# Another layout, and whole rows of 64, for the rotary part of q between two stages of a transformer kernel

## The chip, the cores and the metric

The kernel runs on one core of one Trainium2 chip, as one launch. The metric is the device time of a run in microseconds. Within the core, TensorE (PE in the profile; its weight loads are the row PEld), VectorE (DVE), ScalarE (ACT) and GpSimd (POOL) compute, SyncE (SP) issues every DMA of this kernel, and sixteen DMA engines move the data.

## The reference, cut to what matters

The program is a block of three parts on 1024 tokens of 1024 features: layer 0 (differential attention), layer 1 (attention with compressed keys and queries, "MLA"), and a second block (three mixers and a feed-forward part). Only layer 1 is touched:

```python
def _mla(h, positions, w_in, q_a_norm_g, w_q_b, kv_a_norm_g, w_kv_b, w_out):
    proj = h @ w_in
    q_a, c_kv, k_pe, z = jnp.split(proj, [384, 640, 704], axis=-1)
    q = (_rmsnorm(q_a, q_a_norm_g) @ w_q_b).reshape(b, s, 8, 128 + 64)
    q_nope = q[..., :128]
    q_pe = _rope(q[..., 128:], positions)            # 64 features of each of 8 heads
    k_pe = _rope(k_pe[:, :, None, :], positions)[:, :, 0]   # 64 features, shared by the heads
    kv = (_rmsnorm(c_kv, kv_a_norm_g) @ w_kv_b).reshape(b, s, 8, 128 + 128)
    k_nope, v = kv[..., :128], kv[..., 128:]
    # per head: softmax((q_nope . k_nope + q_pe . k_pe) * 192 ** -0.5) @ v
    o = o.reshape(b, s, 1024) * jax.nn.silu(z)
    return o @ w_out
```

(The sizes are written in for the constants.) `_rope` turns the 64 features of a row in pairs (feature f of the first half with feature f of the second half, f from 0 to 31).

## The kernel before

All arithmetic is fp32; for the matmuls each operand is split into two parts, hi and lo, whose sum is exact, and a product takes three of the four part products (the scores of the rotary part take all four). Activations are kept transposed, features on the partitions, in token halves of 512. A tile has 4 KB a partition; pools hand out a fixed number of buffers for each tag and phase.

Layer 1 runs like this. `lora_norm` makes the normalised q_a and c_kv. `mla_kpe` (L998) makes the rotary part of k for all tokens, stacks hi over lo on 128 partitions and stores it in the DRAM scratch `kd` (L1017); it is read back once into the tile `kpe` (L1142; `h` in the profile, which leaves the digit of the tag `h4` out). `mla_qpe` (L1019) makes the rotary part of q for the heads in two groups of four, g = 0 and 1. A group gives four tiles of 128 partitions, the first and second half of the features (i) by hi and lo (hl); partition 32 x head + f holds feature f. Each tile is stored in the DRAM scratch `qpe` (L1043), which is laid out [head, hl, 64 features, token]: one DMA of 512 KB writes four pieces of 32 rows, one for each head.

Then come eight heads. `mla_head` (L1051) makes q_nope and k_nope of a head, and for hi and for lo it loads the head's 64 rows of `qpe` into a tile of 128 partitions (L1062): one DMA of 512 KB that reads the 64 rows twice, as [2 copies, 64, 1024], so that they stand against the hi rows and against the lo rows of `kpe`. The scores of a query tile are the five matmuls L1093 to L1097 for each half of the keys; L1096 and L1097 use the two loaded tiles. A row maximum on DVE (L737), an exponential on ACT (L741), a scaling on POOL (L1099), transposes on PE (L757), copies to SBUF on ACT and DVE (L761, L169), and the product with v (L192) follow; L1104 multiplies the result by the gate.

While the attention of head h runs, `merge` interleaves v of this head, the preparation of head h + 1 and the modulation vectors of the second block (`modulation`, L298: 48 loads of 512 KB into the three `tb` buffers at L308, and one DVE operation on each, L316 or L318). A scheduler orders the instructions of each engine by its own estimate of the times; each engine, SP too, works through its list in order. SP's DMAs go round eight semaphores, and the next DMA on a semaphore is issued after the last one on it has landed.

Of the kernel before, what the change touches and what calls it, by code (L numbers as in the profile page):

```python
# [44 lines left out]
def alternate(a, b):  # L45
    """steps of a and of b together"""
    for _ in a:
        next(b, None)
        yield
    yield from b  # L50
# [7 lines left out]
def ahead(tc, gen, offset):  # L58
    """steps of gen, scheduled before work that was emitted up to offset instructions earlier"""
    if not offset:  # L60
        yield from gen
        return
    while True:
        with tc.high_priority(offset):
            x = next(gen, drain)
        if x is drain:
            return
        yield x


def some(g, n):
    """n steps of g"""
    for _ in range(n):
        if next(g, drain) is drain:
            return
        yield


def merge(main, fill, lead=0):
    """emit one step of fill after each step of main"""  # L80
    for _ in range(lead):
        next(fill, None)
    for _ in main:
        next(fill, None)
    drain(fill)


def pace(main, total, early, fill, n):
    """steps of early at once, then n steps of fill spread over main, whose steps give their weight"""
    w = done = 0  # L90
    for x in main:
        w += x or 1
        if next(early, 0) == 0:
            while done < n * w / total:
                next(fill, None)
                done += 1
    drain(early)
    drain(fill)


class Net:
# [18 lines left out]
    def load(self, tag, shape, dt=F32):  # L120
        """a tile to be loaded, but not long before its phase"""
        n = self.loads.get((self.phase, tag), 0)
        self.loads[self.phase, tag] = n + 1
        t = self.t(tag, shape, dt)
        if self.phase and n < CAPS[self.phase][tag]:
            first = t[:, 0:1]
            while len(first.shape) > 2:
                first = first[:, :, 0]
            self.nc.gpsimd.tensor_copy(first, self.sign)
        return t  # L130

    def t(self, tag, shape, dt=F32):
        """a tile of 4 KB a partition, seen in the shape"""
        self.n += 1
        t = self.pools[self.phase][tag].tile([128, 1024], dt, tag=f"{tag}{self.phase}", name=f"{tag}_{self.n}")
        dims = "abcd"[:len(shape) - 1]
        t = t[:, 0:math.prod(shape[1:])]
        return t.rearrange(f"p ({' '.join(dims)}) -> p {' '.join(dims)}", **dict(zip(dims, shape[1:])))
# [9 lines left out]
    def c(self, shape, name, dt=F32):  # L148
        """a constant, or columns that stay"""
        r = dt == F32R  # L150
        n = 1 if r else shape[1]
        if name not in self.where:
            self.where[name] = self.used[r]
            self.used[r] += n
        o = self.where[name]
        return self.cr[:, o] if r else self.cf[:, o:o + n]

    def small(self, cols, tag):
        """columns for a short time: the next of a few in turn"""
# [11 lines left out]
    def wblock(self, src, k, m, lo_eng=None):  # L171
        """src: DRAM [k*128, m]; returns [(hi, lo)] per contraction chunk, each [128, m]"""
        return self.wload([src], k, m, lo_eng)

    def wload(self, srcs, k, m, lo_eng=None):
        """blocks of columns side by side"""
# [10 lines left out]
    def mm3(self, out, ws, rs, start=True, stop=True):  # L187
        """out += sum_k ws[k]^T rs[k]; ws, rs: (hi, lo)"""
# [26 lines left out]
    def columns(self, tile_name, width, names):  # L215
        """vectors as columns [128, j]"""
# [23 lines left out]
    def mask_tile(self, name, op, pattern, mult):  # L240
        """0 where the condition holds, else -BIG"""
# [39 lines left out]
    def sigmoid(self, sg, z, src):  # L281
        """sg <- sigmoid(z); src: where |z| is read from (z or its PSUM source)"""
# [15 lines left out]
    def modulation(self, cs, w, bcol, names, acc_tag="t2", w_tag="wr", shared=()):  # L298
        """columns [128, 8] of each 1024 outputs of cs @ w + b; chunks in shared: on ScalarE and GpSimd"""
# [27 lines left out]
    def sum_cols(self, acc, out):  # L327
        """out [128, 8] <- sums over the partitions of acc"""
# [7 lines left out]
    def modulation_first(self, cs, w, bcol, g, nme, acc_tag, w_tag):  # L336
        """as modulation, half of the products on TensorE"""
# [24 lines left out]
    def scale_col(self, g, scale, name):  # L362
        """g * (1 + scale)"""
# [14 lines left out]
    def stat_sum(self, acc):  # L378
        """sum over partitions, on every partition (PSUM)"""
# [10 lines left out]
    def rsqrt_mean(self, out, sums, dim):  # L390
        """(sums / dim + eps)^-1/2"""
# [5 lines left out]
    def stat_end(self, acc, dim):  # L397
        """acc -> (sum over partitions / dim + eps)^-1/2 on every partition, in place"""
        return self.rsqrt_mean(acc, self.stat_sum(acc), dim)

    def new_xt(self, tags):
        """x^T of a token half: 8 chunks [128, 512] in len(tags) tiles"""
# [37 lines left out]
    def operand(self, x, tag="h4", eng=None):  # L440
        """x [128, 512], split"""
# [5 lines left out]
    def rows(self, w, c0, m=128):  # L447
        """loads columns c0.. of w as the rows of a block, by halves of the contraction"""
# [8 lines left out]
    def weights(self, load, early):  # L457
        """operands of two blocks of rows by the number of the product, the first two products' first"""
# [20 lines left out]
    def strassen(self, load, ops, box, tag, early=False):  # L479
        """two blocks of rows times h, [128, 1024] each; early: the products of the first token half, alone,  # L480
        in steps"""
# [31 lines left out]
    def next_h(self, proj, xbox, acc, acol, shift):  # L513
        """ends the projection; h of the next part (fp32, in the place of x), and the operands of its first
        token half"""
# [16 lines left out]
    def turn_ops(self, ops, b11, b12, b21, b22):  # L532
        """operands of a chunk of each half of the contraction, but the first two products'; in place"""
# [11 lines left out]
    def start_pairs(self, pair, n, chunk, ops):  # L545
        """the first pairs of blocks: what needs the first token half, the other operands, the rest"""
# [13 lines left out]
    def load_x(self):  # L560
        """tokens of x"""
# [8 lines left out]
    def turn_x(self, toks):  # L570
        """x^T of the token halves, and their normalisation as rows on every partition"""
# [31 lines left out]
    def rope_half(self, psa, psb, half, outs):  # L603
        """outs: Ah, Al, Bh, Bl views"""
# [15 lines left out]
    def qk_rope(self, w, qcol, kcol, hts, perm=1):  # L620
        """q, k of two 64-wide heads, roped, split and stacked for the scores: kk[s], q[s](hl, q tile)"""
# [56 lines left out]
    def score(self, ps, q, j, kk, ks, stop=True):  # L678
        """ps = q tile j . keys ks, all four products of the parts"""
# [4 lines left out]
    def v_tiles(self, w, cols, k, rs, perm=1, pair=False):  # L684
        """v [key, 128] of the columns, split: [128, hl, 8, 128], or pair: [128, 8, 2, hl, 64]"""
# [31 lines left out]
    def silu_blocks(self, w, cols, hts, box):  # L717
        """silu(h @ w[:, c:c + 128])^T for c in cols, fp32 [128, 1024]"""
# [14 lines left out]
    def exp_row(self, ps, scale):  # L733
        """softmax numerator and reciprocal of its sum"""
# [13 lines left out]
    def pt_fill(self, pts, p, slot, ktiles):  # L748
        """transposes of p[:, k tiles] into column slot; pts = [hi 0-1, lo 0-1, hi 2-3, ..]"""
# [14 lines left out]
    def pv(self, v, pts):  # L764
        """O^T [128, 512]"""
# [5 lines left out]
    def out_proj(self, w, ots, gcol, xs_in, xs_out, half, tags, stats, accs, box):  # L771
        """x' = x + gate * (o @ w) for a token half, in T layout; stats: column factors (or None) of accs"""
# [18 lines left out]
    def keep_o(self, o):  # L791
        """o^T chunk, split"""
# [11 lines left out]
    def load_o(self, od, half, cs, ots, fac=None):  # L804
        """chunks cs of o^T of a token half from DRAM, split"""
# [17 lines left out]
    def last_head(self, att, w0, w1, early, loads, proj, hold=0):  # L823
        """the attention of the last head; fill in its first half (of weight w0): early and the loads of
        the first half's o^T, in its second: the output projection of the first half (but hold steps,
        which come with the loads of the second half's o^T)"""
# [142 lines left out]
    def lora_norm(self, w, c0, n, dim, gcol, hts, tags, box):  # L969
        """rmsnorm of h @ w[:, c0:c0+128n], as (hi, lo) tiles [half][block]"""  # L970
# [28 lines left out]
    def mla_kpe(self, w, c0, hts, kd):  # L999
        """roped k_pe^T stacked [hi (x1, x2); lo (x1, x2)]"""  # L1000
# [16 lines left out]
        nc.sync.dma_start(kd, kpe.bitcast(F32))  # L1017

    def mla_qpe(self, wq, qa, qpe):  # L1019
        """roped q_pe of all heads -> DRAM [head, hl, 64, 1024]"""  # L1020
        nc = self.nc
        for g in range(2):
# [18 lines left out]
            for i in range(2):  # L1041
                for hl in range(2):
                    nc.sync.dma_start(qpe[g * 4:g * 4 + 4, hl, i * 32:i * 32 + 32, :], ab[i][hl].bitcast(F32))  # L1043

    def split_psum(self, ps, dst):
        """dst [128, 2, 512] <- exact parts of ps"""
# [3 lines left out]
    def mla_head(self, h, wq, wkv, qa, ckv, qpe, box):  # L1050
# [9 lines left out]
        for hl in range(2):  # L1060
            t = self.t("h4", [128, S], F32R)
            nc.sync.dma_start(t.bitcast(F32), qpe[h, hl:hl + 1].to_broadcast([2, 64, S]))  # L1062
# [44 lines left out]
    def layer1(self, hts):  # L1107
# [27 lines left out]
        qpe = self.scratch([8, 2, 64, S], "qpe")  # L1135
# [65 lines left out]
    def gelu(self, ps, dst):  # L1201
        """tanh-form gelu of ps into dst (SBUF)"""
# [11 lines left out]
    def mixer_a(self, w, hts, od):  # L1214
        nc, a = self.nc, self.a
        # causal w_sp, transposed and split
# [12 lines left out]
        for b in range(2):  # L1229
# [6 lines left out]
            # v: [s, g, n, c], group norm  # L1236
# [41 lines left out]
    def mixer_b_qk(self, w, p, hts, box):  # L1278
        """q, k of the heads of pair p"""
# [26 lines left out]
    def fold(self, ps, y, e):  # L1306
        """y rows of head e <- sum of the two row halves of ps"""
# [55 lines left out]
    def mixer_c_attention(self, g, d, kk, q, vbox, lse, od):  # L1363
# [4 lines left out]
        for e in range(2):  # L1368
# [61 lines left out]
            # lse = max * scale + ln(sum), 1 / sum; to token order  # L1430
# [17 lines left out]
    def alphas_c(self, lse, fac):  # L1448
        """softmax of lse over the 3 groups, over the softmax sum; [6, 1024] in token order"""
# [80 lines left out]
    def ffn(self, hs, ops):  # L1530
        """the convolved gate and val in pairs of blocks, and their product, kept in DRAM; then the product
        with w_down"""
# [47 lines left out]
    def down(self, half, k1, k2, act, ys):  # L1580
        """x + gate * (act @ w_down) for a token half, in T layout; ys: the chunks before k1"""
# [39 lines left out]
    def finish(self, xt, half):  # L1621
        """rmsnorm of x in token layout, with g_final"""
# [68 lines left out]
```

## Time and profile before

| | |
|---|---|
| median of 3 runs | 3095.03 us (3091.07 to 3096.7) |
| span of the profiled execution | 3102.5 us |
| granted TensorE clock, mean over the span | 0.929 |
| layer 1, from the store of `kd` to the end of the last head | about 1046 to 1620 us of the span |
| DMA issues of the program / of `qpe` and `kd` | 1073 / 8 stores and 16 loads, 1 store and 1 load, 512 KB each |

The span is 7.5 us longer than the median of the runs, and 5.8 us longer than the longest of them. A profile gives the time at which an instruction ran, not what the DMA engines did for it; when a transfer landed is read from the instruction that waited for it. In a timeline row the bracket is the idle time of the engine before the instruction, and what ended it. In a row of windows, "PEclk" is the granted clock and "DMA share" the mean busy share of the sixteen DMA engines.

### The profile page before, as it was taken

The numbers are of one execution on the slowest core, as the hardware profiler recorded it, in microseconds if no ns is written. First come the engines' busy times: TensorE is split into PE (matmuls) and PEld (weight loads), VectorE is DVE, ScalarE is ACT, GpSimd is POOL, SyncE is SP. The second block draws the span as 40 slices with busy tenths as digits, with TensorE's granted clock in tenths as the row PEclk, the third lists the DMA queues.
The fourth block names the chain that finished last, engine by engine and source line by source line (L and its number), as shares of the span: only waits on it lengthen the run. The fifth ranks groups of instructions, "written<-read, shape, count | busy, mean of one in ns | idle before, by whom it ended". The sixth has DMA issues, their size and how long they took to land. (4 is left out here: it accounts for less than half of the span.)

```text
span 3102.5 us, 34630 instructions
## 1 busy us (share of the span) xinstructions
PE 2673.2 (86%) x12023; PEld 2154.1 (69%) x12023; DVE 2110.7 (68%) x2888; ACT 1434.4 (46%) x2609; POOL 1292.2 (42%) x775
## 2 busy tenths in 40 slices
PE   7899999999989957778789689888887999998897
PEld 4677777777767746567667567777675777776776
DVE  7787778766653365555566756377876888889865
ACT  5455554556444423334345444366743444444332
POOL 2323333223353522112124333244545877787761
PEclk8999999999999978889899899999998999998998
DMA  7433333224441352321334235533361222224664
GB/s 268 132 93 96 105 94 90 72 67 118 122 122 53 117 178 78 100 83 53 103 106 131 68 81 82 107 82 100 97 195 46 77 82 75 82 89 149 210 213 153
DMA packets 316225, 338.90 MB, mean 109 GB/s; under 512 B 37060, under 2 KB 239892, under 8 KB 316052
## 3 DMA queue, kind: packets, MB, share of 16 engines
q1 hardware_dynamic: 316052, 336.69, 37.0%
q8 instruction: 96, 1.57, 0.2%
q14 instruction: 77, 0.63, 0.1%
HBM read 231.17 MB, written 60.89 MB: 94 GB/s over the span
## 5 line engine op out<-in xcount | busy, mean ns | idle before, releaser
L192 PE MATMUL m<-h,wh 128*128 128x512 f32 x4744 | 1399.6, 404 | 59.3 <-ACT wh L183 18.6
L192 PEld LDWEIGHTS m<-h,wh 128*128 128x128 f32 x4744 | 912.1, 195 | 269.3 <-ACT wh L183 21.0
L192 PE MATMUL m<-h,wl 128*128 128x512 f32 x1472 | 590.3, 403 | 10.1 <-POOL wl L169 10.0
L169 POOL TENSOR_TENSOR wl<-wr,wh 128x1024 fp32r<-128x1024 f32 (+1 forms) x146 | 329.4, 2263 | 577.6 <-PE m L192 184.4
L761 ACT CAST pt<-m 128x256 fp32r<-128x256 f32 (+1 forms) x632 | 221.2, 369 | 367.8 <-DVE pt L169 192.1
L192 PEld LDWEIGHTS m<-h,wl 128*128 128x128 f32 x1472 | 286.5, 195 | 75.3 <-POOL wl L169 12.5
L169 DVE TENSOR_TENSOR pt<-m,pt 128x256 fp32r<-128x256 f32 (+2 forms) x652 | 256.8, 416 | 103.2 <-ACT pt L761 81.7
L741 ACT ACTIVATE e<-s,cf 128x1024 f32<-128x1024 f32 x192 | 214.8, 1120 | 163.6 <-DVE cf L738 140.2
L737 DVE TENSOR_REDUCE cf<-s 128x1 f32<-128x1024 f32 x192 | 232.6, 1218 | 70.6 <-PE s L682 38.6
L757 PE MATMUL m<-cr,e 128*128 128x128 f32 x1240 | 197.1, 285 | 61.3 <-DVE t L1104 31.4
L757 PEld LDWEIGHTS m<-cr,e 128*128 128x128 f32 x1240 | 155.3, 147 | 89.4 <-issue 53.4
L192 PE MATMUL s<-h,wh 128*128 128x512 f32 x720 | 182.8, 399 | 35.9 <-DVE h L169 17.1
L865 POOL TENSOR_SCALAR e<-e,cf 128x1024 f32<-128x1024 f32 x64 | 82.0, 1281 | 303.8 <-DVE cf L742 286.6
L681 PE MATMUL s<-kk,qq 128*128 128x512 f32 (+3 forms) x376 | 154.0, 415 | 51.6 <-ACT e L741 22.4
L1527 DVE SCALAR_TENSOR_TENSOR e<-z,cf,e 128x1023 f32<-128x1023 f32 (+1 forms) x88 | 175.8, 2008 | 24.8 <-ACT e L1525 24.6
L183 ACT CAST wh<-wr 128x1024 fp32r<-128x1024 f32 (+2 forms) x134 | 122.2, 915 | 145.5 <-PE m L192 67.6
L192 PE MATMUL m<-pt,v 128*128 128x512 f32 x768 | 187.7, 394 | 0.8 <-DVE pt L169 0.6
L192 PEld LDWEIGHTS s<-h,wh 128*128 128x128 f32 x720 | 136.3, 191 | 71.8 <-DVE h L169 18.9
L192 PEld LDWEIGHTS m<-pt,v 128*128 128x128 f32 x768 | 143.9, 189 | 31.6 <-DVE pt L169 1.5
L1099 POOL TENSOR_SCALAR e<-e,cf 128x1024 f32<-128x1024 f32 x64 | 72.8, 1141 | 213.8 <-DVE cf L742 210.0
L682 PE MATMUL s<-kk,qq 128*128 128x512 f32 (+3 forms) x376 | 146.0, 396 | 0.2 <-DMA qq<-pt 0.2
L169 DVE TENSOR_TENSOR wh<-wl,wh 128x512 fp32r<-128x512 f32 x90 | 120.6, 1358 | 19.1 <-ACT wh L443 19.0
(368 smaller groups left out, 4582.3 us busy)
## 6 DMA issues: line engine op xcount, KB each, us to landing
wr<-in_w_out_dram SPq DMA_DIRECT2D x48, 512.0 KB
tb<-in_w_ada_dram SPq DMA_DIRECT2D x48, 512.0 KB
wr<-in_w_up_dram SPq DMA_DIRECT2D x47, 512.0 KB
wr<-in_w_in_dram SPq DMA_DIRECT2D x45, 512.0 KB
qq<-ab SPq DMA_DIRECT2D x144, 128.0 KB
wr<-in_ada_w_dram SPq DMA_DIRECT2D x32, 512.0 KB
tf<-act SPq DMA_DIRECT2D x30, 512.0 KB
wr<-in_w_down_dram SPq DMA_DIRECT2D x30, 512.0 KB
```

Of the source, the lines that this page charges most:

```text
L169: (eng or self.nc.vector).tensor_sub(lo, src, hi.bitcast(F32))
L183: nc.scalar.copy(hi, raw)
L192: self.nc.tensor.matmul(out, l, r, start=start and n == 0, stop=stop and n == last)
L681: nc.tensor.matmul(ps, q(0, j), kk[:, ks], start=True, stop=False)
L682: nc.tensor.matmul(ps, q(1, j), kk[:, ks], start=False, stop=stop)
L737: nc.vector.reduce_max(nm, ps, axis=AX, negate=True)
L741: nc.scalar.activation(e, ps, AF.Exp, bias=nm, scale=scale, accum_out=sm)
L757: nc.tensor.transpose(ps[:, i], p[:, kt * 128:(kt + 1) * 128], self.ident)
L761: nc.scalar.copy(hi, ps[:, i:i + m])
L865: nc.gpsimd.tensor_scalar(e1, e1, r1, self.neglam, ALU.mult, ALU.mult)
L1099: nc.gpsimd.tensor_scalar(e, e, r, 1.0, ALU.mult, ALU.mult)
L1527: nc.vector.scalar_tensor_tensor(t[:, sh:], u[:, 0:S - sh], col(i), t[:, sh:], ALU.mult, ALU.add)
```

## The change

The scratch `qpe` becomes [hl, head x 32 features, half i, token]. A group's tile of 128 partitions is then stored to 128 rows that lie 8 KB apart, and a head's 64 rows for hi or lo lie together, in the order (f, i) where it was (i, f). A load is written as two DMAs of 64 rows, one for the upper and one for the lower 64 partitions. So that k stands in the same order, `kd` is written by four DMAs of 32 rows. The arithmetic is the same. The docstrings and comments are gone from the new file, which shifts lines and nothing else; they are left out here.

```diff
@@ mla_kpe @@
-        nc.sync.dma_start(kd, kpe.bitcast(F32))
+        rows = kd.rearrange("(d f i) t -> d i f t", d=2, i=2)
+        for d in range(2):
+            for i in range(2):
+                nc.sync.dma_start(rows[d, i], kpe[64 * d + 32 * i:64 * d + 32 * i + 32].bitcast(F32))
@@ mla_qpe @@
             for i in range(2):
                 for hl in range(2):
-                    nc.sync.dma_start(qpe[g * 4:g * 4 + 4, hl, i * 32:i * 32 + 32, :], ab[i][hl].bitcast(F32))
+                    rows = qpe[hl, g * 128:g * 128 + 128, i]
+                    nc.sync.dma_start(rows, ab[i][hl].bitcast(F32))
@@ mla_head @@
             t = self.t("h4", [128, S], F32R)
-            nc.sync.dma_start(t.bitcast(F32), qpe[h, hl:hl + 1].to_broadcast([2, 64, S]))
+            rows = qpe[hl, h * 32:h * 32 + 32].rearrange("f i t -> (f i) t")
+            for d in range(2):
+                nc.sync.dma_start(t[64 * d:64 * d + 64].bitcast(F32), rows)
             qp.append(t)
@@ layer1 @@
-        qpe = self.scratch([8, 2, 64, S], "qpe")
+        qpe = self.scratch([2, 8 * 32, 2, S], "qpe")
```

The lists of the engines hold the same instructions as before, but for 19 more DMAs on SP, and differ in order at some places. On SP, the first place is where `kd` and the first group of `qpe` are stored (L1017, L1043) between loads of weights (`wr`), stores of the gate (`zd`) and the read-back of `kd`. Before:

```order
L1017 DMA kd<-e_8019 128x1024
L182 DMA wr_8490<-in_w_in_dram 128x8x128
L1142 DMA h_1347_8590<-kd 128x1024
L182 DMA wr_8601<-in_w_q_b_dram 128x3x128
L182 DMA wr_8637<-in_w_kv_b_dram 128x2x128
L182 DMA wr_8708<-in_w_kv_b_dram 128x2x128
L1043 DMA qpe<-pt_8234 4x32x1024
L1043 DMA qpe<-pt_8236 4x32x1024
L1043 DMA qpe<-pt_8235 4x32x1024
L1120 DMA zd<-z_8276 128x1024
L1043 DMA qpe<-pt_8237 4x32x1024
```

And of the change (its L1020, L1047, L1126 and L1148 are L1017, L1043, L1120 and L1142 of before):

```order
L1020 DMA kd<-e_8019 32x1024 x4
L1148 DMA h_1347_8593<-kd 128x1024
L182 DMA wr_8493<-in_w_in_dram 128x8x128
L182 DMA wr_8604<-in_w_q_b_dram 128x3x128
L182 DMA wr_8642<-in_w_kv_b_dram 128x2x128
L182 DMA wr_8713<-in_w_kv_b_dram 128x2x128
L1047 DMA qpe<-pt_8237 128x1024
L1047 DMA qpe<-pt_8239 128x1024
L1047 DMA qpe<-pt_8238 128x1024
L1047 DMA qpe<-pt_8240 128x1024
L1126 DMA zd<-z_8279 128x1024
```

The store of `kd` is four rows of the list, the read-back moved ahead of one weight load, and the shape of a store of `qpe` went from four pieces of 32 rows to 128 rows. The second place on SP is the load of a head, here of the third (`h_1507` for hi and `h_1508` for lo; `tb` are the modulation's loads). Before:

```order
L1062 DMA h_1507_9446<-qpe 128x1x1024
L1062 DMA h_1508_9448<-qpe 128x1x1024
L182 DMA wr_10236<-in_w_q_b_dram 128x3x128
L308 DMA tb_11727<-in_w_ada_dram 128x1024
L308 DMA tb_11962<-in_w_ada_dram 128x1024
```

And of the change (L1068 is L1062 of before):

```order
L1068 DMA h_1507_9453<-qpe 64x1024
L1068 DMA h_1508_9456<-qpe 64x1024
L1068 DMA h_1507_9453<-qpe 64x1024
L1068 DMA h_1508_9456<-qpe 64x1024
L182 DMA wr_10247<-in_w_q_b_dram 128x3x128
L308 DMA tb_11744<-in_w_ada_dram 128x1024
L308 DMA tb_11981<-in_w_ada_dram 128x1024
```

Here two rows became four, and what follows them kept its order.

## The prediction

> **What bounds the kernel now.** I read the page first, for the engine that is busy most:
>
> ```profile
> PE 2673.2 (86%) x12023; PEld 2154.1 (69%) x12023; DVE 2110.7 (68%) x2888; ACT 1434.4 (46%) x2609; POOL 1292.2 (42%) x775
> h<-qpe SPq DMA_DIRECT2D x16, 512.0 KB
> qpe<-pt SPq DMA_DIRECT2D x8, 512.0 KB
> ```
>
> TensorE is busy for 86% of the span, so time can be won only where PE stands still or runs at a lower clock. The change touches layer 1, so the next view is the windows over its eight heads, over one head, and over pieces of it:
>
> ```profile
> core 0: us, PE busy (x) PEld busy (x) DVE busy (x) ACT busy (x) POOL busy (x), PEclk, DMA share, GB/s
> 1120.00:1620.00 500.00, 387.01 (x1880) 317.00 (x1879) 275.27 (x561) 195.86 (x457) 93.95 (x86) 0.88 0.30 96
> 1318.00:1322.00 4.00, 0.00 (x0) 0.00 (x0) 0.00 (x0) 0.00 (x0) 0.00 (x0) 0.50 0.13 51
> 1322.00:1328.00 6.00, 5.65 (x16) 4.49 (x17) 0.00 (x0) 0.94 (x2) 0.36 (x1) 0.52 0.02 8
> 1328.00:1357.00 29.00, 29.00 (x152) 24.41 (x151) 19.19 (x44) 16.72 (x41) 8.12 (x8) 1.00 0.11 37
> 1378.00:1386.00 8.00, 0.00 (x0) 0.00 (x0) 1.53 (x2) 0.00 (x0) 0.00 (x0) 0.50 0.13 53
> ```
>
> In the 500 us of the heads PE is idle for 113 us (500 less 387.01), and its clock is 0.88. It isn't idle all along: from 1328 to 1357 it is busy without a gap at full clock, with DVE and ACT well below it. It stops in blocks. In two of these, 1318 to 1322 and 1378 to 1386, no engine but DVE does anything, and the DMA engines are busy to 0.13: 2 of 16 would give 0.125. So everything waits for a transfer that uses two engines' worth of the sixteen. The waits of 1085 to 1620 name it, with what ended each:
>
> ```profile
> PE s L1097 <- DMA h<-qpe: 36.6, 4, 10.0
> PE m L757 <- DVE t L1104: 31.4, 2, 15.8
> PE s L1094 <- DVE h L169: 23.4, 2, 17.5
> PE m L192 <- DVE pt L169: 20.6, 3, 20.0
> PE s L1093 <- DVE h L169: 8.8, 1, 8.8
> PE m L704 <- ACT tf L700: 6.8, 1, 6.8
> DVE z L318 <- DMA tb<-in_w_ada_dram: 87.4, 9, 20.0
> DVE pt L169 <- DMA qpe<-pt: 8.3, 1, 8.3
> ```
>
> Four heads wait for the load of `qpe` itself (36.6 us). The waits for DVE are the less plain ones: DVE was waiting in turn for a `tb` load. Their timelines show why; first a head of the first kind:
>
> ```profile
> 1299.17 1.63 SPq L1062 DMA_DIRECT2D h<-qpe  x2
> 1313.14 0.40 PE L1096 MATMUL s<-h,h 128*128 128x512 f32 x1
> 1322.35 0.79 PE L1097 MATMUL s<-h,h 128*128 128x512 f32 x1 [8.81 <-DMA h<-qpe]
> ```
>
> The two loads are issued at 1299.17; PE gets to the tile of hi at 1313.14 and is held by the tile of lo until 1322.35, 23.2 us after the issue. At the 51 to 53 GB/s of the windows above, 2 x 512 KB take 20 us, so that is the transfer's own rate. Now one of the second kind:
>
> ```profile
> 1232.51 1.63 SPq L1062 DMA_DIRECT2D h<-qpe  x2
> 1239.02 0.74 DVE L316 TENSOR_SCALAR z<-tb,cf 128x1024 f32<-128x1024 f32 x1
> 1241.31 19.48 SPq L308 DMA_DIRECT2D tb<-in_w_ada_dram  x4
> 1242.87 0.16 DVE L1166 TENSOR_TENSOR cf<-cf 128x8 f32<-128x8 f32 x1
> 1259.15 1.28 DVE L318 SCALAR_TENSOR_TENSOR z<-tb,cf,z 128x1024 f32<-128x1024 f32 x1 [16.12 <-DMA tb<-in_w_ada_dram]
> 1261.18 1.09 PE L757 MATMUL m<-cr,e 128*128 128x128 f32 x4 [15.58 <-DVE t L1104]
> ```
>
> A `tb` load issued at 1241.31, nine us behind the two loads of `qpe`, is there only at 1259.15. The part of it that falls to the two slow engines queues behind `qpe`. DVE, which works in order, stands at L318, and behind it stand L1104 and the copies that PE needs.
>
> For comparison, a load of the same 512 KB whose outermost dimension is 128, issued while little else was in flight, and the cast that waited for it:
>
> ```profile
> 1051.02 0.38 SPq L182 DMA_DIRECT2D wr<-in_w_in_dram  x1
> 1055.34 1.05 ACT L183 CAST wh<-wr 128x1024 fp32r<-128x1024 f32 x1 [2.53 <-DMA wr<-in_w_in_dram]
> ```
>
> It took at most 4.3 us, where one load of `qpe` takes some 10 us in its turn.
>
> **The change part by part.**
>
> *The loads.* `qpe` is read as [2 copies, 64, 1024] now; 64 rows after the change. If the leading 2 is what binds a load to two engines, four loads of 256 KB use all sixteen. Their time isn't in the trace. The short bound is the best rate that the windows show (250 GB/s, quoted below), 4.2 us for 1 MB. The long one is that each of the four takes as long as the whole 512 KB above, 4 x 4.3 = 17.3 us. I take 7 us, near the short one, since several loads overlap in the windows. SP's part is two more issues of about 0.5 us a head, and PE waits 13 us before it needs the first tile (1299.17 to 1313.14), so that is covered.
>
> The Trainium skill ("DMA: Bandwidth & Descriptors", "Why a DMA increments its semaphore by 16 and not by 1") says that a transfer runs on the largest number of engines, up to 16, that divides the outermost dimension other than 1 of both sides: by it 2 now and 16 after, and the sum is the forecast's. The 0.13 agrees. The same page ("Rules for kernel authors") speaks against the way it is done: two transfers to disjoint halves of the partitions serialise, and one of 128 partitions is better. No run here shows that; what it would make of the time is the second rival.
>
> What goes with it on PE, from the rows above: 36.6 (the four direct waits), 31.4 (two heads behind L1104), 17.5 (one of the two before L1094) and 20.0 (the longest before L192): **105.5 us**. What is late next, in a head with `tb` loads, is the buffer: the first of the four is free when L316 ends (1239.76). At 3 to 4.3 us a load it lands at 1243 to 1244, and DVE wants it at 1243.03. That leaves about 1 us in each of four heads. In the second head the list of SP now puts three more `tb` loads before the load of `qpe`; I allow 3 us there.
>
> *The stores.* A store's four pieces of 32 rows become 128 rows.
>
> ```profile
> 1074.00:1080.00 6.00, 4.35 (x20) 3.27 (x18) 3.02 (x4) 1.29 (x2) 3.49 (x2) 1.00 0.26 103
> 1116.59 8.47 SPq L1043 DMA_DIRECT2D qpe<-pt  x3
> 1143.04 0.42 DVE L169 TENSOR_TENSOR pt<-m,pt 128x256 fp32r<-128x256 f32 x1 [8.34 <-DMA qpe<-pt]
> 1144.69 0.48 PE L704 MATMUL m<-cr,tf 128*128 128x128 f32 x1 [6.81 <-ACT tf L700]
> ```
>
> While the first group's stores drain, the DMA share is 0.26, four of sixteen. The second group's stores still hold `pt` buffers 18 us after their last issue; DVE waits 8.34 us for one and PE 6.81 us behind it. On sixteen engines they land some 4 us after their issue, long before 1134. **6.8 us** go.
>
> *The beginning of the heads.*
>
> ```profile
> 1085.00:1100.00 15.00, 7.19 (x31) 5.59 (x29) 13.04 (x12) 4.05 (x8) 4.07 (x2) 0.84 0.71 250
> 1069.20 0.69 DVE L610 TENSOR_TENSOR tf<-m,tb 128x512 f32<-128x512 f32 x1 [7.68 <-DMA qpe<-pt]
> 1081.45 0.73 PE L192 MATMUL m<-kk,wh 128*128 128x512 f32 x2 [3.09 <-ACT z L725]
> 1092.17 0.68 DVE L610 TENSOR_TENSOR tf<-m,tb 128x512 f32<-128x512 f32 x1
> 1107.38 1.28 DVE L169 TENSOR_TENSOR h<-m,h 128x512 fp32r<-128x512 f32 x2
> ```
>
> The waits before L1093 (8.8) and 5.9 of those before L1094 (23.4 less 17.5) have another cause: from 1085 to 1100 DVE itself is busy 13 of 15 us. They don't go, but they move: DVE's earlier waits for the stores (7.68 at 1069.20) and the 3.09 us of PE behind them end sooner, so the DVE chain from 1092.17 to 1108.7, 16.5 us long, can start when PE delivers, some 4 us earlier. I take **5 us** (bounds 0 and 10).
>
> *The clock.* After each stop PE runs at half clock: in 1322 to 1328, after the stop at L1097, PE is busy for 5.65 us at 0.52, which is 2.7 us of work lost. There are nine such stops (four direct, four behind DVE, one behind the stores): 24 us. Some of it hides other engines' catching up; I take **18 us** (bounds 0 and 24).
>
> *The rest.* `kd` is written by four DMAs, three issues of about 0.4 us more; SP then waits for them before the read-back. PE has work there and the first use of `kpe` is at L1096, 60 us later: nothing, and 3 us if that cover were gone. The lists of later stages differ in places by neighbours that changed order: nothing, within 5 us either way.
>
> *The sum.* 105.5 + 6.8 + 5 + 18 = 135.3 us. Against it: 4 x 1 and 3 us of new waits, and about 3 us for waits of PE on ACT and DVE that the stops cover now (from 1328 to 1357 there are none). That leaves 125 us: a span of 3102.5 - 125 = 2977.5. The span is 7.5 us above the median of the runs, so I predict **2970 us** as the median.
>
> **The rivals.**
>
> 1. *The wait is for the `tb` buffers, not for slow engines.* There are only three, and the four issues from 1241.31 stretch over 19.48 us. Then only the direct waits and the stores' go: 36.6 + 6.8 and five stops' clock, 13: 57 us, 3038. Against it: DVE waits at 1243 for a load issued at 1241.31, which had its buffer, and the DMA share is 0.13 meanwhile. Chance 0.04.
> 2. *Half-partition transfers run one after the other*, at 4.3 us each. The load is there after 17.3 us and an issue, PE waits at about 1318 and not 1322: 4 us won in each of four heads, some 6 in each of the four with `tb` (17.3 against 23.2 us of queue), 6.8 and 5 at the stores, and little clock: 16 + 24 + 11.8 + 5 = 57 us, less if the waits stay apart; 3038 as well. For it: no load to 64 partitions of this size is in the trace. Chance 0.10. This is the second rule of the Trainium skill above ("DMA: Bandwidth & Descriptors", "Rules for kernel authors"), carried over to this kernel.
> 3. *The split doesn't spread the transfer*: rows that lie together might be handled as one run. Then the load keeps its 23 us. No change from that, and the stores' 6.8 + 5 + 2: 3081, or 3095 if these don't spread either. Chance 0.03 in all for "no change".
> 4. *Slower*: as 3, but with four transfers in a row on the same two engines, each with an end of its own. In the trace the first tile is there 14 us after the issue at the latest (1313.14) and its data take 10, so an end costs up to 4 us. PE or DVE already waits there in all eight heads, so two more ends a head add at most 2 x 4 x 8 = 64 us; half of that gives 3127. It decides when the DMA share in the loads' stretch stays at 0.13. Against it: DMAs with 128 rows outermost do reach 0.71. Chance 0.04.
> 5. *More than forecast*: the clock's 24 us in full, 10 at the beginning, no new waits: 105.5 + 6.8 + 10 + 24 = 146, 2949. Chance 0.09.
>
> **How the numbers follow.** The forecast has 0.70 (gains from 100 to 140 us, 2955 to 2995). For the range I add rival 5 and the upper part of the forecast's neighbours towards rival 2, where the loads take 10 to 14 us: 2945 to 3015 leaves out most of rivals 1 to 4. A difference of 0.2%, 6 us, is about what a measurement of this kernel can tell from no change. Faster has the forecast, rivals 1, 2 and 5 and half of 3: 0.94 (rounded down); within 0.2%: 0.02; slower: 0.04.
>
> **What would show it.** In the new profile: the waits of PE on `h<-qpe` at 3 us or less in total; DVE at L318 waiting for `tb` under 15 us in total where it is 87.4; no wait on `qpe<-pt` in the heads; a clock of 0.95 or more over the eight heads, and these some 390 us long and not 500. The DMA share within 8 us of a load's issue should be above 0.3. If the share stays at 0.13, rivals 3 and 4 have it; if the direct waits go and DVE's waits at L318 stay, rival 1; if both are halved, rival 2. The prediction would be wrong above all if PE, no longer stopped by DMAs, stopped for DVE or ACT in every head.

## The result and the profile after

| | before | change |
|---|---|---|
| median of 4 runs each | 3093.2 us (3091.07 to 3096.7) | 2962.88 us (2959.48 to 2965.16) |
| ratio, 95% interval | | 0.9579 (0.9565 to 0.9592) |
| span of the profiled execution | 3102.5 us | 2962.4 us |
| granted clock over the span | 0.929 | 0.951 |

The change is 130.3 us faster; 125 were forecast. From the page of the change, the lines that answer to those of before:

```profile
span 2962.4 us, 34674 instructions
PE 2646.8 (89%) x12023; PEld 2136.0 (72%) x12023; DVE 2118.1 (71%) x2888; ACT 1437.1 (49%) x2609; POOL 1291.4 (44%) x775
h<-qpe SPq DMA_DIRECT2D x32, 256.0 KB
qpe<-pt SPq DMA_DIRECT2D x8, 512.0 KB
```

The work of DVE, ACT and POOL is what it was. PE is busy 26.4 us less for the same 12023 matmuls, as its clock is higher over the span; some 6 us of that lie in the mixers behind the layer (99.82 and 93.76 us, last section) and not in the heads. The windows of the change (us, then busy time of PE, PEld, DVE, ACT, POOL, then granted clock, DMA share and GB/s) over the heads, and over two moments after a head's four loads were issued at 1184.25:

```profile
core 0: us, PE busy (x) PEld busy (x) DVE busy (x) ACT busy (x) POOL busy (x), PEclk, DMA share, GB/s
1120.00:1490.00 370.00, 353.32 (x1811) 289.76 (x1810) 262.95 (x542) 190.08 (x445) 91.38 (x83) 1.00 0.38 114
1186.00:1190.00 4.00, 4.00 (x27) 3.50 (x26) 3.17 (x8) 3.31 (x8) 1.17 (x2) 1.00 0.92 236
1190.00:1191.00 1.00, 1.00 (x6) 0.84 (x5) 1.00 (x3) 0.08 (x1) 0.66 (x1) 1.00 0.34 87
...
1184.25 2.86 SPq L1068 DMA_DIRECT2D h<-qpe  x4
```

In the heads PE idles for 16.7 us of 370, where it idled for 113 of 500, and the clock is 1.00 where it was 0.88. While the loads run, the DMA engines are busy to 0.92 at 236 GB/s; before it was 0.13 at 51. From 1190 on the rate falls, about 6 us after the first issue. The longest waits of PE in the heads, 1085 to 1490, and DVE's wait for `tb`:

```profile
PE s L1100 <- DVE h L169: 8.8, 4, 6.2
PE s L1099 <- ACT e L741: 3.4, 2, 2.9
PE m L192 <- DVE cf L738: 2.5, 2, 2.3
PE s L1099 <- DVE h L169: 2.4, 1, 2.4
PE m L757 <- DVE v L169: 1.9, 1, 1.9
...
DVE z L318 <- DMA tb<-in_w_ada_dram: 2.7, 6, 0.7
```

No wait on `h<-qpe` and none on `qpe<-pt` is left. DVE's waits for `tb` fell from 87.4 to 2.7 us, though no `tb` load was touched by the change. Where the gain lies is seen from the last of the five score matmuls, of before and of the change (count, then min/median/max ns, then the first and the last start):

```profile
L1097 PE MATMUL s<-h,h x128: 388/389/797, 1119.1 to 1610.5; 128*128 128x512 f32 x128
L1103 PE MATMUL s<-h,h x128: 387/389/628, 1100.6 to 1480.9; 128*128 128x512 f32 x128
```

The first head gets there 18.5 us earlier, the last one 129.6 us earlier: all of the gain of the timed runs is there when the heads end. (The profiled spans differ by 140.1 us. The other 10 are not the change's; see the end.)

### The profile page after: what moved, and what is told of

The parts are those of the page before. It is cut to its first block, busy times and chain, and to the rows that moved or that the text cites. A ratio compares the mean times of both kernels' runs of the same rounds, so it can differ in the third digit from the quotient of the medians.

```text
span 2962.4 us, 34674 instructions
## 1 busy us (share of the span) xinstructions
PE 2646.8 (89%) x12023; PEld 2136.0 (72%) x12023; DVE 2118.1 (71%) x2888; ACT 1437.1 (49%) x2609; POOL 1291.4 (44%) x775
## 5 line engine op out<-in xcount | busy, mean ns | idle before, releaser
L192 PE MATMUL m<-h,wh 128*128 128x512 f32 x4744 | 1398.8, 404 | 62.3 <-ACT wh L183 16.2
L192 PEld LDWEIGHTS m<-h,wh 128*128 128x128 f32 x4744 | 910.4, 194 | 270.9 <-ACT wh L183 18.8
L192 PE MATMUL m<-h,wl 128*128 128x512 f32 x1472 | 589.8, 402 | 8.8 <-POOL wl L169 8.8
L169 POOL TENSOR_TENSOR wl<-wr,wh 128x1024 fp32r<-128x1024 f32 (+1 forms) x146 | 330.5, 2270 | 479.0 <-ACT wh L183 183.7
L192 PEld LDWEIGHTS m<-h,wl 128*128 128x128 f32 x1472 | 286.9, 195 | 73.9 <-POOL wl L169 11.2
L169 DVE TENSOR_TENSOR pt<-m,pt 128x256 fp32r<-128x256 f32 (+2 forms) x652 | 256.3, 416 | 83.1 <-ACT pt L761 70.8
L192 PE MATMUL s<-h,wh 128*128 128x512 f32 x720 | 183.3, 400 | 36.4 <-DVE h L169 17.1
L192 PE MATMUL m<-pt,v 128*128 128x512 f32 x768 | 188.7, 395 | 1.0 <-DVE pt L169 0.5
L192 PEld LDWEIGHTS s<-h,wh 128*128 128x128 f32 x720 | 136.9, 192 | 72.7 <-DVE h L169 18.6
L192 PEld LDWEIGHTS m<-pt,v 128*128 128x128 f32 x768 | 144.4, 190 | 32.3 <-DVE pt L169 1.6
L169 DVE TENSOR_TENSOR wh<-wl,wh 128x512 fp32r<-128x512 f32 x90 | 121.7, 1370 | 19.4 <-ACT wh L443 19.2
```

Of the source, the lines that this page charges most:

```text
L169: (eng or self.nc.vector).tensor_sub(lo, src, hi.bitcast(F32))
L192: self.nc.tensor.matmul(out, l, r, start=start and n == 0, stop=stop and n == last)
```

## The experiments

The theory is the forecast's: a transfer whose outermost dimension is 2 runs on two of the sixteen DMA engines, one with 4 on four, and what queues behind it on these engines is late as well. The rivals: the number of loads or their data matter and not the outermost dimension; reading the same rows twice (the step of 0) is the slow part; transfers to half of the partitions cost something of their own.

The experiments were run in four sets, each on a chip of its own. The kernel before took 3092.1 us in the first set and 3114.0, 3115.9 and 3114.0 us in the others, so the time of a kernel is compared within its set. A time forecast from the 3093.2 us of the result has to be read some 20 us higher in the later sets. The position of the last score matmul serves across sets: the change has it at 1480.9, 1482.7 and 1480.4 us in its three profiles.

### The loads alone, the stores alone

`e1_loads_only` is the kernel before with the load alone split; `qpe` and `kd` are stored as before. `e2_stores_only` is the change with the load of before, copies outermost.

```diff
 e1_loads_only (against before)
-            nc.sync.dma_start(t.bitcast(F32), qpe[h, hl:hl + 1].to_broadcast([2, 64, S]))
+            for d in range(2):
+                nc.sync.dma_start(t[64 * d:64 * d + 64].bitcast(F32), qpe[h, hl])
 e2_stores_only (against the change)
-            rows = qpe[hl, h * 32:h * 32 + 32].rearrange("f i t -> (f i) t")
-            for d in range(2):
-                nc.sync.dma_start(t[64 * d:64 * d + 64].bitcast(F32), rows)
+            both = qpe.rearrange("l (h f) i t -> l h (f i) t", f=32)
+            nc.sync.dma_start(t.bitcast(F32), both[hl, h:h + 1].to_broadcast([2, 64, S]))
```

> The kernel before with one edit: each load of a head's rows is two DMAs of 64 rows; scratch, stores and the store of k as before. Theory (a transfer whose outermost dimension is 2 runs on two of the sixteen engines, and the loads were such transfers): the direct waits on the load and DVE's waits for tb go, the stores' waits stay (8 us at L169, 7 to 12 us in all). 2980 us, 2970 to 2990. Rival (the stores on four engines carry a good part of the gain): above 3000. Rival (the tb buffers): no faster than 3040.

> The change with its loads undone: new layout, stores of 128 rows, k stored by four DMAs, and a head's load as one DMA over [2 copies, 64, 1024] again. Theory: PE's direct waits on the load and DVE's waits of some 16 us for tb are back in all heads, only the stores' part is won: 3080 us, 3070 to 3090. Rival (contiguous rows alone speed the load): below 3020.

Measured: `e1_loads_only` 2986.48 us (2982.22 to 2987.49), ratio 0.966 (0.9645 to 0.9674); `e2_stores_only` 3078.0 us (3070.89 to 3088.69), ratio 0.9955 (0.9942 to 0.9968). The split of the loads is worth 105.6 us of the 130, the stores' form 14.1 us alone; after the split the rest of the change adds some 24 us (2986.48 to 2962.88), and why it is worth 10 us more there was not separated. First two of `e2_stores_only`'s waits of PE and one of DVE in the heads:

```profile
PE s L1102 <- DMA h<-qpe: 40.9, 5, 9.6
PE m L757 <- DVE t L1109: 37.5, 3, 15.5
DVE z L318 <- DMA tb<-in_w_ada_dram: 69.4, 6, 16.2
```

The direct waits and the waits for `tb` are back with the load's form alone. What the stores' form leaves is at the beginning of the heads. In `e1_loads_only`, from 1040 to 1120:

```profile
PE s L1094 <- DVE h L169: 8.6, 1, 8.6
PE s L1095 <- DVE h L169: 5.9, 1, 5.9
PE m L192 <- ACT z L725: 2.9, 1, 2.9
DVE tf L610 <- DMA qpe<-pt: 7.6, 1, 7.6
DVE tf L613 <- DMA qpe<-pt: 4.5, 1, 4.5
```

DVE waits 12.1 us for buffers that the old stores still hold. In the change neither of these two waits is there, PE's at L192 is gone, and its L1099 (the L1094 here) waits 2.4 us and not 8.6. PE's wait of 6.8 us before L704, which the forecast put down to the stores, does not appear in `e1_loads_only` either, nor does DVE's of 8.3 us at L169, which had been expected to stay. Both are absent from `e2_stores_only` as well: they took the old loads and the old stores together, and either edit alone removes them.

### Is it the outermost dimension, or the repeated rows?

`e3_copies_inside` keeps one DMA for 128 partitions and the step of 0, but turns them round: 64 rows, then 2 copies, then 1024 (`kd` is stored in the order that goes with it). `e4_far_copies` has an outermost 2 without a step of 0: each tile is stored twice, and a load reads two blocks of 64 rows that lie apart.

```diff
 e3_copies_inside (against the change)
-        rows = kd.rearrange("(d f i) t -> d i f t", d=2, i=2)
+        rows = kd.rearrange("(f i d) t -> d i f t", d=2, i=2)
...
-            rows = qpe[hl, h * 32:h * 32 + 32].rearrange("f i t -> (f i) t")
-            for d in range(2):
-                nc.sync.dma_start(t[64 * d:64 * d + 64].bitcast(F32), rows)
+            rows = qpe[hl, h * 32:h * 32 + 32].rearrange("f i (o t) -> (f i) o t", o=1)
+            nc.sync.dma_start(t.bitcast(F32), rows.to_broadcast([64, 2, S]))
```

> The change with each pair of half loads as one DMA of 128 partitions that reads every row twice in turn, [64 rows, 2 copies, 1024]; k is stored in the matching order (f, i, copy). Theory (the outermost dimension counts, 64 here): as fast as the change, 2963 us within 8, 16 DMAs fewer. Rival (reading the same rows twice, the step of 0, is what made the load slow): 3080. Rival (two half loads run one after the other and cost more than one whole): the load lands sooner, but no wait on it is left in the change, so at most 3 us faster.

> Every tile of q is stored twice, in two copies that lie apart, and a head's load is one DMA over [2, 64, 1024] with no step of 0: no row is read twice, but the outermost dimension is 2. Theory: the load is as slow as before the change, DMA share 0.13 behind it, and the time is 3080 us (3070 to 3100; eight more stores of 512 KB add at most 10). Rival (the step of 0): 2963 to 2975.

Measured: `e3_copies_inside` 2957.25 us (2952.97 to 2966.65), ratio 0.9563 (0.9547 to 0.9579); `e4_far_copies` 3082.65 us in a single run, within its range. The waits of `e4_far_copies`, then a window of it soon after the two loads of a head (issued at 1278.32), and below it the same of `e3_copies_inside` (issued at 1233.67):

```profile
PE s L1099 <- DVE h L169: 44.4, 3, 22.1
PE s L1102 <- DMA h<-qpe: 34.7, 4, 10.2
PE m L757 <- DVE t L1109: 30.8, 2, 15.4
DVE z L318 <- DMA tb<-in_w_ada_dram: 78.8, 6, 20.6
...
1280.00:1283.00 3.00, 3.00 (x18) 2.60 (x17) 2.29 (x5) 2.24 (x6) 0.10 (x1) 1.00 0.14 51
...
1235.00:1238.00 3.00, 3.00 (x19) 2.57 (x17) 2.37 (x5) 1.88 (x4) 0.00 (x0) 1.00 0.96 265
```

Two copies read with a step of 0 are as fast as the change when 64 rows stand outside them; two blocks of different memory are as slow as before when 2 stands outside. The DMA share goes with it: 0.14 at 51 GB/s in the one, 0.96 at 265 in the other. Neither the step of 0 nor the number of DMAs is the cause. The outermost dimension is.

### Four instead of two

`e8_four` reads one DMA with 4 outermost: every tile is stored twice, so that a load finds four blocks of 32 rows; `kd` is stored as before, and there are eight more stores than in the change.

```diff
 e8_four (against the change)
-                    rows = qpe[hl, g * 128:g * 128 + 128, i]
-                    nc.sync.dma_start(rows, ab[i][hl].bitcast(F32))
+                    for d in range(2):
+                        nc.sync.dma_start(qpe[d, i, hl, g * 128:g * 128 + 128], ab[i][hl].bitcast(F32))
...
-            rows = qpe[hl, h * 32:h * 32 + 32].rearrange("f i t -> (f i) t")
-            for d in range(2):
-                nc.sync.dma_start(t[64 * d:64 * d + 64].bitcast(F32), rows)
+            both = qpe.rearrange("d i l (h f) t -> l h (d i) f t", f=32)
+            nc.sync.dma_start(t.bitcast(F32), both[hl, h])
```

> One DMA of 128 rows for a load, the outermost dimension 4 (32 rows each; the scratch holds every tile twice, so no step is 0; twice the stores, 16 DMAs). Theory (the outermost dimension sets how many engines a transfer runs on): two loads take about half of the 23 us of before, 10 to 12 us; most of the waits go, what is left is a few us a head: 2985 us (2970 to 3005). Rival (anything but a single block of contiguous rows is slow): 3080 us. Rival (four blocks are as good as one): 2963 us.

Measured: 3018.42 us (3015.75 to 3020.65), ratio 0.969 (0.9675 to 0.9704). Here is a window of `e8_four` after the two loads of a head, and below it the waits of PE (three rows) and of DVE in the heads:

```profile
1257.00:1263.00 6.00, 6.00 (x32) 5.07 (x31) 3.68 (x9) 3.38 (x8) 1.85 (x2) 1.00 0.26 78
...
PE s L1096 <- DVE h L169: 26.7, 3, 13.4
PE m L757 <- DVE t L1106: 16.2, 2, 8.2
PE s L1099 <- DMA h<-qpe: 1.8, 2, 1.6
DVE z L318 <- DMA tb<-in_w_ada_dram: 37.5, 5, 12.0
```

The share is 0.26, four of sixteen: 0.13, 0.26 and 0.92 for an outermost 2, 4 and 64. The direct waits are all but gone (1.8 us), since PE comes to the tiles only some 14 us after the issue (1299.17 to 1313.14 in the kernel before). The `tb` loads queued behind still cost DVE 37.5 us, and PE stands behind DVE: 26.7 us in the row that was 8.8 in the change, and 16.2 us. The last score starts at 1517.1, 36.2 us after the change's 1480.9. 22 us had been expected: the waits behind `tb` are longer than the few us a head of the forecast. The time as measured lies above its range of 2970 to 3005; less the 20.8 us by which the kernel before was slower in this set it is 2997.6 us, inside. Both rivals (3080 and 2963 us) are out either way.

### Which heads, and what the narrow load delays

In these two only some heads load as before. Heads 3, 5 and 7 are those in which PE itself waited for the load; in 2, 4 and 6 DVE waited for `tb`.

```diff
 e5_narrow_357 (against the change)
+            if h in (3, 5, 7):
+                both = qpe.rearrange("l (h f) i t -> l h (f i) t", f=32)
+                nc.sync.dma_start(t.bitcast(F32), both[hl, h:h + 1].to_broadcast([2, 64, S]))
+            else:
...
 e6_narrow_246: the same, with
+            if h in (2, 4, 6):
```

> The change, but heads 3, 5 and 7 load with the copies outermost (one DMA, [2, 64, 1024]) as before. Theory (a load whose outermost dimension is 2 runs on few engines and is late at those places where it was late before): the odd heads get back TensorE's own waits on h<-qpe of before at heads 3, 5, 7, 8.8 + 8.5 + 10.0 = 27 us, and some 8 us of clock behind them: 2998 us (2990 to 3005), with h<-qpe named as the releaser of TensorE and tb<-in_w_ada_dram hardly longer than in the change. Rival (only the number of narrow loads counts, each worth the same, 115 / 7 us): 3 x 16 = 49 us: 3012 us.

> The change, but heads 2, 4 and 6 load with the copies outermost as before. Theory: here the loads of the modulation weights stand behind the narrow loads on the same queue, VectorE waits for tb and TensorE behind VectorE: 15.6 + 15.8 + 17.5 = 49 us as before, and some 8 us of clock: 3020 us (3010 to 3030); the releasers named are VectorE's instructions and tb<-in_w_ada_dram, and TensorE has no wait of its own on h<-qpe. Rival (only the number counts): 49 us: 3012 us. Rival (a narrow load delays only the head that reads it): TensorE waits on h<-qpe, and the tb loads wait no longer than in the change.

Measured: `e5_narrow_357` 3017.89 us (3015.54 to 3018.1), ratio 0.9687 (0.9672 to 0.9701); `e6_narrow_246` 3026.74 us (3019.64 to 3031.59), ratio 0.9712 (0.9689 to 0.9735). For `e5_narrow_357`, the waits of PE on the load and of DVE on `tb`, and the last score matmul:

```profile
PE s L1107 <- DMA h<-qpe: 26.5, 3, 9.8
DVE z L318 <- DMA tb<-in_w_ada_dram: 3.4, 6, 0.8
...
L1107 PE MATMUL s<-h,h x128: 387/389/795, 1100.1 to 1517.1; 128*128 128x512 f32 x128
```

And for `e6_narrow_246`:

```profile
PE m L757 <- DVE t L1114: 31.0, 2, 15.6
PE s L1104 <- DVE h L169: 22.6, 2, 16.7
DVE z L318 <- DMA tb<-in_w_ada_dram: 48.1, 3, 16.1
...
L1107 PE MATMUL s<-h,h x128: 387/389/632, 1101.6 to 1530.5; 128*128 128x512 f32 x128
```

The same edit shows as two different waits. In the odd heads it is PE's own, three times, 26.5 us (27 expected). In the even heads PE has no wait on the load at all; DVE waits for `tb` three times, 48.1 us (49 expected), and PE behind DVE. By the last score the odd heads cost 36.2 us (35 expected) and the even ones 49.6 us, where 57 were expected. PE's two rows are 44.8 us longer there than in the change (53.6 against 8.8), which leaves some 5 us for the clock where 8 were expected. The times as measured put the odd heads above their range (2990 to 3005) and the even ones inside theirs (3010 to 3030). Less the 20.8 us of this set they are 2997.1 us, which was forecast as 2998, and 3005.9 us, 4 us below its range. That every narrow load costs the same 16 us fits the even heads (49) but not the odd ones, 13 us off.

### A second profile of before

`e7_before_again` is the kernel before, unchanged, in the set of the last three.

> The kernel before, unchanged, for a second profile of it. If the 9 us by which the first profiled execution was longer than the timed median belong to that execution, this span is near 3092 us and the mixers' part is as long as in the change; if a profile costs this kernel some 9 us, this span is again near 3102 us.

Measured: a span of 3115.3 us and a time of 3116.96, beside a median of 3114.0 us of the kernel before in this set. Neither case of the expectation came: the span is longer than both, on a chip where the kernel before ran some 20 us slower, and a profile does not cost 9 us here. As the chip was another one, the run does not say why the first profiled execution was longer than its timed runs. Its last score starts at 1607.5 us, 3 us before that of the first profile, although the span is 12.8 us longer: what differs between the two lies behind the heads.

### One DMA for 128 partitions, or two for 64

`e3_copies_inside` had come out 5.6 us below the change. It ran twice more beside the change (`e10_copies_again` with `e9_change_again`, `e12_copies_third` with `e11_change_third`, without edits to either).

> The change, unchanged, on the same chip as the next kernel. If the price of a chip's slower state lies outside the heads, its distance to the kernel before is again 130 us (ratio 0.957 to 0.959).

> One DMA of 128 rows for a load, the copies inside (64 rows, 2 copies with a step of 0, 1024), beside the change. Theory (both are spread over all 16 engines; 16 DMAs and their issue fewer on SP): within 3 us of the change, or up to 6 us faster (16 issues of some 0.45 us on the queue, hidden for the most part). Rival (reading each row twice in turn costs something against two blocks): slower by over 3 us.

> The change once more, beside the next kernel. Expected at 0.957 to 0.959 of the kernel before.

> One DMA of 128 rows for a load, the copies inside, once more beside the change; it was 5.7 and 10.1 us below the change in two calls, with intervals that overlap. Theory (two DMAs to the two halves of the partitions cost nothing that can be measured against one to all 128): within 6 us of the change. Rival (halves cost a few us at the beginning of the heads, where the DMA engines are busiest): 5 to 10 us below the change again.

| set | change | copies inside | difference |
|---|---|---|---|
| result (change), first set (copies inside) | 2962.88 us, 0.9579 (0.9565 to 0.9592) | 2957.25 us, 0.9563 (0.9547 to 0.9579) | 5.6 us |
| third set | 2982.35 us, 0.9568 (0.9549 to 0.9588) | 2972.21 us, 0.9556 (0.9537 to 0.9575) | 10.1 us |
| fourth set | 2974.77 us, 0.9552 (0.953 to 0.9574) | 2965.63 us, 0.9533 (0.9511 to 0.9555) | 9.1 us |

Copies inside is below the change three times out of three, though the intervals overlap each time. The expectations missed by little: 10.1 us lie outside both the theory and the rival of `e10_copies_again`, 9.1 us are the rival's in `e12_copies_third`, and the two repeats of the change came out at 0.9568 and 0.9552, just below 0.957 to 0.959. The last score matmul of `e9_change_again` and of `e10_copies_again`:

```profile
L1103 PE MATMUL s<-h,h x128: 387/389/632, 1098.4 to 1482.7; 128*128 128x512 f32 x128
...
L1102 PE MATMUL s<-h,h x128: 387/389/628, 1097.9 to 1476.3; 128*128 128x512 f32 x128
```

Here 6.4 us are won by the end of the heads; in the other two pairs of profiles it is 1.8 us (1480.9 to 1479.1) and 3.4 us (1480.4 to 1477.0). So copies inside wins 2 to 6 us in the part that it touches. The rest of the differences in the table lies behind the heads, in a part that varies by itself (see the end). Whether the 2 to 6 us come from the transfers or from SP's list, which has 16 DMAs fewer and another order at the beginning of the heads, was not separated. What is settled is that the halves do not take 4.3 us each, one after the other: by the forecast's second rival that would have left 57 us of the gain and not 130.

## Why the prediction was right

**The bound and the mechanism.** The forecast read a share of 0.13 as two engines of sixteen, and the `tb` waits as loads queued behind on these two. Both hold: the share goes with the outermost dimension (0.13, 0.26, 0.92), and narrow loads put into heads 2, 4 and 6 alone bring back 48.1 us of DVE's waits for `tb`. The kernel before shows how such a wait ends, here the stop for the `tb` load issued at 1241.31 (DVE goes on at 1259.15):

```profile
1245.00:1250.00 5.00, 0.61 (x5) 0.30 (x3) 0.00 (x0) 0.00 (x0) 0.00 (x0) 0.93 0.69 202
1250.00:1255.00 5.00, 0.00 (x0) 0.00 (x0) 0.00 (x0) 0.00 (x0) 0.00 (x0) 0.50 0.56 160
1255.00:1259.00 4.00, 0.00 (x0) 0.00 (x0) 0.00 (x0) 0.00 (x0) 0.00 (x0) 0.50 0.13 51
```

The `tb` loads first move on many engines, up to 0.69; in the last four microseconds before the wait ends only two engines' worth, 0.13, is still at work. That agrees with their last parts standing behind `qpe` on two engines; which engines these are, no view shows.

The Trainium skill ("DMA: Bandwidth & Descriptors", "Why a DMA increments its semaphore by 16 and not by 1") has the rule that the number of engines is the largest up to 16 that divides the outermost dimension other than 1 of both sides. `e8_four` at 0.26 and `e4_far_copies`, slow without a step of 0, agree with it.

**The loads, 105.5 us.** Right. The rows of 36.6 and 31.4 us and the stalls of 17.5 and 20.0 us have no counterpart in the change, and the split alone won 105.6 us. That these two agree to 0.1 us is chance: the second figure has some of the clock in it, and PE's 6.8 us before L704, and lacks what the old stores still held up.

**The stores, 6.8 us, and the beginning, 5 us.** Wrongly divided, and too small together. PE's 6.8 us before L704 go with either edit alone, so the stores add nothing there once the loads are split. Their own part is the chain at the beginning. From `e1_loads_only` to the change, 8.6 to 2.4 us at the first score and 2.9 to 0 at L192 make 9.1 us; a wait for ACT's `e` of 4.8 us a little later goes as well (the row was 8.2 us, and is 3.4). It follows a wait of 6.1 us of DVE for `tb`; such waits add up to 11.0 us in `e1_loads_only`, though its expectation had them gone, and to 2.7 us in the change. The last score shows the whole of it, here both lines of `e1_loads_only`:

```profile
PE s L1094 <- ACT e L741: 8.2, 3, 4.8
...
L1098 PE MATMUL s<-h,h x128: 387/389/632, 1111.7 to 1497.0; 128*128 128x512 f32 x128
```

That is 11.1 us behind the change at the first head and 16.1 at the last; the timed runs of the two, from different sets, are 23.6 us apart. The step that was mis-sized is "They don't go, but they move". The first of the two waits did go for the most part, from 8.8 us before to 2.4 (2.9 in `e2_stores_only`, 8.6 in `e1_loads_only`, so it goes with the stores); the second stayed, 5.9 and 6.2 us. With the 3.1 us at L192 the beginning gave 9.5 us, where 5 were taken.

**The clock, 18 us.** About right. In the heads PE was busy 387.01 us for 1880 recorded matmuls, and is now 353.32 us for 1811. Per matmul that is 0.206 and 0.195 us, and over 1880 of them some 20 us (an estimate, since the two windows don't hold quite the same matmuls).

**New waits, 10 us against.** Right in sum, not in kind. The 1 us in each of four heads and the 3 us in the second head are 2.7 us in all, DVE's at L318, where 7 were allowed. All of PE's waits in the heads add up to 136.9 us before (1085 to 1620) and to 28.0 in the change (1085 to 1490). Without the 105.5, the 6.8 and the 6.4 us of the first score that went, 18.2 us of before are left, so 9.8 us are new. The longest row among them is the 2.5 us for DVE's `cf`; those for ACT's `e` and DVE's `v` in the list above were there before, with 4.2 and 1.9 us.

**The load's time, 7 us taken.** The runs show only that it is short enough, since nothing waits for the loads any more; the rate falls from 236 to 87 GB/s about 6 us after the first issue, and by then about 1 MB has been moved. That is near the short one of the bounds of 4.2 and 17.3 us.

**The sum.** 125 us forecast, 130.3 measured. By the rows, waits of 112.0 us went net (136.9 less 28.0, and the 3.1 at L192), where 107.3 were forecast; the difference is the beginning. With the clock's some 20 us that makes 132, an estimate, beside the 129.6 us at the last score. The span of the change was forecast as 2977.5 us, from a profile of before that ran longer than its timed runs; it came out at 2962.4, half a microsecond below the median. The forecast took 7.5 us off for this without a reason; that the excess lay for the most part in a stretch behind the heads, where this kernel varies by itself, is what the last section makes likely.

**The rivals.** The `tb` buffers (1) are out: `tb` loads with the same three buffers wait 2.7 us. Halves in turn (2) are out at the price it gave, by the 0.92 and by `e3_copies_inside`. The Trainium skill ("DMA: Bandwidth & Descriptors", "Rules for kernel authors") advises against two transfers to disjoint halves, since both run on the same sixteen engines. In this case one transfer was better by 2 to 6 us in the heads, while the split itself won more than 100. The 4.3 us for each half in turn were the forecast's own price. No spread (3) and slower (4) are out by the share. More than forecast (5), 2949, was not reached: PE keeps 16.7 us of idle time in the heads.

## What to carry to other kernels

Read the DMA share in the stretch in which everything waits: 0.13 on 16 engines is a transfer on two of them, and the shape to look for is a small outermost dimension, such as a broadcast written with the copies outside. Turn it round (rows outside, copies inside) or split it; either gave back over 100 us here. A narrow transfer also holds up the wide ones queued behind it, so the wait may stand under the name of a load that is itself in order: more of it stood under `tb` (87.4 us) than under `qpe` (36.6 us).

## What was not expected of the hardware

The same kernel differed by 12 to 23 us between sets of runs on different chips, and not in the part that the change touches. Here is a stretch of the mixers after layer 1, with about the same number of matmuls, in the profile of the change and in that of `e9_change_again`, the same kernel on another chip:

```profile
1747.00:1855.00 108.00, 93.76 (x511) 79.58 (x510) 64.01 (x88) 47.80 (x77) 32.91 (x33) 0.95 0.61 103
...
1747.00:1873.00 126.00, 100.32 (x504) 85.02 (x505) 67.13 (x91) 49.55 (x78) 33.32 (x34) 0.85 0.62 89
```

It takes 18 us longer at a clock of 0.85 instead of 0.95. In `before` it takes 115 us at 0.90:

```profile
1878.00:1993.00 115.00, 99.82 (x505) 83.36 (x504) 64.02 (x88) 46.73 (x75) 32.91 (x33) 0.90 0.60 100
```

So most of the 10 us by which the two profiled spans differ beyond the heads lie here (115 against 108), in a stretch that varies by itself. Why the clock is lower there, and whether it is the chip, stays open.
